# A bf16 head that also prepares fp16 weights: one scale for each half of w's columns, with the work on w dealt out anew between ScalarE and VectorE

## The chip, the cores and the metric

The kernel runs on one core of a Trainium2 chip. The core has a matrix engine (TensorE, PE in the profile; its weight loads are PEld), VectorE (DVE), ScalarE (ACT), GpSimd (POOL) and SyncE (SP, which here only issues DMAs). The metric is the time of one execution on the device in microseconds.

## The reference

```
B, S, D = 8, 2048, 2048          # x: (B, S, D) and w: (D, D), float32, normal draws
cs = np.cumsum(x, axis=1)
diff = cs - np.concatenate([zeros, cs[:, :-1, :]], axis=1)
return np.matmul(diff, w).astype(np.float32)
```

The difference of a running sum with itself, one step back, is x again, so the kernel computes the product of x, as 16384 rows of 2048, with w.

## The kernel before, in words

The 16384 rows are 128 row tiles of 128. All but the first four are multiplied in fp16 by a Winograd scheme (seven block products in place of eight, on two levels for most of the work), whose block sums need x and w scaled to fp16. The scheme is not part of the change; what it needs of w is. In its four blocks, B11 and B21 are the upper and lower row halves of w's left 1024 columns, B12 and B22 those of the right 1024; T1 to T4 are differences of the blocks.

**The head.** While w arrives, the first four row tiles (PLAIN = 4) are multiplied plainly in bf16, so that TensorE has work. w comes as 32 tiles of 128 rows by 1024 columns, float32, 512 KB each: `fetch(h, ko)` loads tile ko (0 to 15) of column half h, first all of the left half, then all of the right. x's four row tiles come in four quarters of 512 columns (`load_x`), placed between the loads of w; `cast_x` turns a quarter into bf16 in two instructions on VectorE, `turn_x` transposes it on TensorE into PSUM bank 7, eight 128x128 transposes for two row tiles at a time, and `turned` copies the result out. In the lists `loads` and `turns`, quarters 1, 2 and 3 are loaded ahead of tiles 2, 5 and 9, and turned at tiles 2 and 3, 5 and 6, 9 and 10.

`taken(h, ko)` does two things with a tile of w that has landed: ScalarE casts it to bf16 into one of seven ring buffers `wb` (L259), and VectorE takes the largest magnitude of each partition (L262). `plain(h, r, ko)` multiplies row tile r with it (L275), one 512-column matmul for each PSUM bank, seven for a tile of the left half, eight for the right: bank 7 is needed for the transposes, so the eighth product of the left half is left for later. The last four tiles (KQ = 4) of each half are run row by row, so that `plain_out` can copy a finished row's banks out on ScalarE (L295) while the next row is multiplied. The right half uses the same banks, so its first tile waits for those copies. AHEAD = 3 right-half tiles are fetched and cast before this.

**The scale.** When all 32 tiles are in, VectorE reduces the 32 maxima (L366), GpSimd takes the maximum over the partitions (L367, `partition_all_reduce`), and two small VectorE instructions give uw and its reciprocal uinv (L369, L371). GpSimd then issues seven stores (`put`, L285) for finished rows. `block` turns a float32 tile of w, in place, into a scaled fp16 tile: VectorE does it for B11, B21 and B12 (L382), 24 instructions, ScalarE for most of B22 (L386).

**Rows of x in the scheme.** For each row tile t, `weigh` takes row sums of magnitudes on ScalarE (L123, two 1024-column instructions, each with a read of the accumulator), `scale_of` turns them into a scale on VectorE (L139, L141), `unit_of` multiplies it by uw on GpSimd (L147), `narrow` casts the scaled row to fp16 on ScalarE (L158), and `turn` transposes it by DMA (L171). `keep` on ScalarE (L581) and `add` on VectorE (L584) bring a product out of PSUM, times the row tile's unit, into an output buffer.

**Order.** `after` chains every instruction behind the last one on its engine, so each engine runs in the order in which the Python code calls the helpers, and an instruction that waits holds up all that follow on that engine. Between the engines only the data count. Behind the head stand, on ScalarE: the row sums and the narrowing of row tile 4, the copies of row 0 (banks 0 and 1), the row sums of tile 6, the copies of row 1 (banks 2 and 3), and so on. TensorE goes on with `left_over(bank(2))`, the 16 matmuls of the product that was left (L400), into bank 2, and then with the scheme (L554, L573). Row tile 5 is loaded into xP's space once rows 0 and 1 are done with it (L432).

**The end.** The last group's final products are run in the order written out in END_ORDER: in its last line a bank q is closed by P4.p7, then read by `add.C21h1.q` on VectorE and by `keep.C21h0` on ScalarE; the last add, `add.C21h0.x`, needs that keep's result.

Of the kernel before, what the change touches and what calls it, by code (L numbers as in the profile page):

```python
# [10 lines left out]
def kernel(  # L11
# [6 lines left out]
    nc = tc.nc  # L18
# [23 lines left out]
    PLAIN = 4  # L42
    KQ = KO // 4
# [26 lines left out]
    uw = const.tile([P, 1], f32, name="uw")  # L70
    uinv = const.tile([P, 1], f32, name="uinv")
# [60 lines left out]
    def scale_of(t):  # L132
        if t < END:
            m2 = sums_of.pop(t)
            m, s, u = (m2[:, i : i + 1] for i in (2, 3, 4))
# [44 lines left out]
    with ExitStack() as head:  # L180
# [10 lines left out]
        wmax = first.tile([P, 2 * KO], f32, name="wmax")  # L191
        wred = first.tile([P, 1], f32, name="wred")
# [62 lines left out]
        def taken(h, ko):  # L255
            wt = whole[ko % KH][:, ko // KH, h, :]
            i = h * KO + ko
            b = wb[h, ko] = turn_of(ring)
            after("act", lambda: nc.scalar.copy(b, wt))  # L259
            after(  # L260
                "dve",
                lambda: nc.vector.tensor_reduce(  # L262
                    wmax[:, i : i + 1], wt, AX.X, MAX, apply_absolute_value=True
                ),
            )

# [31 lines left out]

        for i in range(WARM):
# [6 lines left out]
        AHEAD = 3  # L306
# [59 lines left out]
        after("dve", lambda: nc.vector.tensor_reduce(wred, wmax, AX.X, MAX))  # L366
        whole_max = nc.gpsimd.partition_all_reduce(uw, wred, P, bass_isa.ReduceOp.max)  # L367
        after(
            "dve", lambda: nc.vector.tensor_scalar(uw, uw, TINY, 1.0 / TOP, MAX, MUL)  # L369
        )  # L370
        after("dve", lambda: nc.vector.reciprocal(uinv, uw))  # L371
# [4 lines left out]


        def block(dst, a, h, k, engine):
            src = whole[k][:, a, h, :].rearrange("p (n c) -> p n c", c=NB)
            if engine == "dve":  # L380
                after(
                    "dve", lambda: nc.vector.tensor_scalar(dst[k], src, uinv, None, MUL)  # L382
                )
            else:
                after(
                    "act", lambda: nc.scalar.activation(dst[k], src, COPY, scale=uinv)  # L386
                )
# [8 lines left out]
        def left_over(ps):  # L396
# [12 lines left out]
            after("act", lambda: nc.scalar.activation(c, ps, COPY, scale=uw))  # L409
# [3 lines left out]
        for k in range(4):  # L413
            block(B11, 0, 0, k, "dve")
# [23 lines left out]
        for k in range(4, KH):  # L438
# [809 lines left out]
```

## Time and profile before

| | |
|---|---|
| median of 3 runs | 1454.4 us (1453.6 to 1454.54) |
| profiled execution | 1453.86 us, of which the span from the first to the last instruction is 1452.1 us |
| granted TensorE clock | 1.000 over the span |
| busy share of the span | PE 99%, DVE 92%, ACT 67%, POOL 3% |
| DMA | 351.59 MB, 242 GB/s on the mean; 404 GB/s from 10 to 20 us |
| chain that ended last | PE 96%, DMA 2%, DVE 1% of the span |

The profiled execution lies inside the three runs; 1.8 us of it are outside the span. Times inside the profile are counted from the span's start. A row of the timeline gives the start, the length, the engine, the line in the code, the operation, what it writes and reads, the shape and how many instructions are merged into the row; in brackets stands how long the engine was idle before it and what ended that. A matmul's record is 0.38 us long, but the next one starts before it ends, so rows of matmuls are counted by their starts. An engine's neighbouring instructions overlap by about 0.09 us in the same way.

### The profile page before, as it was taken

To read this page: it belongs to the slowest core of one execution; us is meant where nothing else is said; L and a number is where in the kernel's file an instruction comes from. 1 tells how busy PE (TensorE), PEld (TensorE's weight loads), DVE (VectorE), ACT (ScalarE), POOL (GpSimd) and SP (SyncE) were. 2 spreads that over 40 slices of the span, in tenths; PEclk is the share of its full clock that TensorE was granted. 3 is DMA by queue.
4 is the path that set the end of the run, shared out by engine and by line. 5 is a ranking of instruction groups with operands and counts; after the bars stand their busy time and mean duration, and the time that the engine had idled before them with its cause. 6 is when DMAs were issued, how large, how long until landed. Compare 5 with 4: busy or idle time off the path is not lost.

```text
span 1452.1 us, 20113 instructions
## 1 busy us (share of the span) xinstructions
PE 1438.4 (99%) x6673; PEld 651.6 (45%) x6679; DVE 1332.9 (92%) x2301; ACT 967.7 (67%) x1446; POOL 47.2 (3%) x136
## 2 busy tenths in 40 slices
PE   8999999999999999999999999999999999999998
PEld 3444444444444444444444444444444444444443
DVE  7998999999999999999999999999999999999998
ACT  5887566776666676666666667666667766666662
POOL 0111000000000000000000000000000000000000
PEclk9999999999999999999999999999999999999999
DMA  9999788898888888888898888998878898888983
GB/s 363 370 237 299 194 220 240 239 261 235 231 238 231 250 245 235 233 238 237 249 253 225 232 236 234 265 235 239 229 231 244 249 235 239 222 245 246 252 203 123
DMA packets 377752, 351.59 MB, mean 242 GB/s; under 512 B 274800, under 2 KB 274800, under 8 KB 377520
## 3 DMA queue, kind: packets, MB, share of 16 engines
q1 hardware_dynamic: 377088, 348.47, 84.9%
q0 software_dynamic: 560, 1.84, 0.4%
q8 instruction: 52, 0.85, 0.2%
q14 instruction: 52, 0.43, 0.1%
HBM read 150.99 MB, written 134.22 MB: 196 GB/s over the span
## 4 chain that ended last, share of the span: by engine, by line
PE 96%; DMA 2%; DVE 1%; ACT 0%; issue 0%; SPq 0%; ACTq 0%
PE b L573 61%; PE b L554 33%; PE b L275 2%; DMA W<-in_w_dram 2%; DVE c L584 1%; DMA W<-in_x_dram 0%; ACT wb L259 0%; PE b L400 0%; ACT o L295 0%; SPq L219 0%; ACT c L581 0%; SPq L253 0%; DVE x L544 0%; ACTq L259 0%
## 5 line engine op out<-in xcount | busy, mean ns | idle before, releaser
L584 DVE SCALAR_TENSOR_TENSOR c<-b,of,c 128x512 f32<-128x512 f32 x790 | 573.9, 747 | 73.1 <-PE b L573 62.5
L554 PE MATMUL b<-W,x 128*128 128x512 f16 x2144 | 506.6, 379 | 0.0
L581 ACT ACTIVATE c<-b,of 128x512 f32<-128x512 f32 x492 | 312.6, 680 | 227.3 <-PE b L573 115.7
L573 PE MATMUL b<-W,x 128*128 128x512 f16 x1904 | 454.9, 379 | 0.0
L158 ACT ACTIVATE F<-F,of 128x1024 f16<-128x1024 f32 x246 | 282.2, 1147 | 175.4 <-DVE of L141 173.2
L573 PEld LDWEIGHTS <-x 128*128 128x128 f16 x2500 | 244.6, 98 | 295.7 <-issue 1.5
L554 PEld LDWEIGHTS <-x 128*128 128x128 f16 x2144 | 209.8, 98 | 253.0
L123 ACT ACTIVATE waste<-F 128x1024 uint8<-128x1024 f32 x246 | 259.3, 1054 | 4.9 <-DMA F<-in_x_dram 2.8
L573 PEld LDWEIGHTS <-inner 128*128 128x128 f16 x1644 | 160.9, 98 | 194.0
L573 PE MATMUL b<-W,inner 128*128 128x512 f16 x940 | 241.2, 379 | 0.0
L544 DVE TENSOR_TENSOR x<-x,x 128x1024 f16<-128x1024 f16 (+1 forms) x390 | 227.4, 583 | 3.2
L573 PE MATMUL b<-flow,x 128*128 128x512 f16 x588 | 150.9, 379 | 0.0
L573 PE MATMUL b<-inner 128*128 128x512 f16 x472 | 121.1, 379 | 0.0
L895 DVE TENSOR_TENSOR flow<-W 128x2048 f16<-128x2048 f16 x88 | 107.0, 1216 | 0.0
L988 DVE TENSOR_TENSOR b<-b,c 128x512 f32<-128x512 f32 x116 | 80.6, 695 | 13.5 <-PE b L573 13.4
L147 POOL TENSOR_SCALAR of<-of,uw 128x1 f32<-128x1 f32 x124 | 42.0, 357 | 1305.4 <-DVE of L139 703.1
L895 DVE TENSOR_TENSOR flow<-W,inner 128x2048 f16<-128x2048 f16 x58 | 70.8, 1221 | 0.0
L981 ACT COPY c<-b 128x512 f32<-128x512 f32 x58 | 33.4, 576 | 52.2 <-PE b L573 49.6
L275 PE MATMUL b<-wb,xP 128*128 128x512 bf16 x234 | 55.1, 383 | 6.6 <-ACT wb L259 5.2
L544 DVE TENSOR_TENSOR inner<-x 128x512 f16<-128x512 f16 x117 | 49.4, 422 | 2.9 <-DMA x<-F 0.9
L981 ACT COPY b<-b 128x512 f32<-128x512 f32 x87 | 51.2, 588 | 0.0
L544 DVE TENSOR_TENSOR inner<-x,inner 128x512 f16<-128x512 f16 x117 | 49.3, 421 | 2.0
(61 smaller groups left out, 524.3 us busy)
## 6 DMA issues: line engine op xcount, KB each, us to landing
F<-in_x_dram SPq DMA_DIRECT2D x246, 512.0 KB, 5.1
out_dram<-c SPq DMA_DIRECT2D x492, 256.0 KB, 3.0
W<-in_w_dram SPq DMA_DIRECT2D x32, 512.0 KB, 9.7
W<-in_x_dram SPq DMA_DIRECT2D x16, 256.0 KB, 7.3
x<-F SPq DMA_TRANSPOSE x246, 3.3
out_dram<-o POOLq DMA_DIRECT2D x5, 256.0 KB, 4.1
out_dram<-o SPq DMA_DIRECT2D x5, 256.0 KB, 3.4
xP<-in_x_dram SPq DMA_DIRECT2D x1, 1024.0 KB, 5.1
```

The costliest lines, as they stand in the source:

```text
L123: lambda: nc.scalar.activation(waste, where[t][i], ABS, scale=1.0 / ROW, accum_out=sums_of[t][:, i : i + 1],),
L147: after("pool", lambda: nc.gpsimd.tensor_scalar(u, m, uw, None, MUL))
L158: lambda: nc.scalar.activation(narrowed(t)[:, ds(i * NH, NH)], where[t][i], COPY, scale=s),
L275: lambda: nc.tensor.matmul(ps[r][n], xP[:, r, ko, :], wb[h, ko][:, ds(n * NB, NB)], start=(ko == 0), stop=(ko == KO - 1),),
L544: after("dve", lambda: nc.vector.tensor_tensor(dst.all, p.all, q.all, op))
L554: said = nc.tensor.matmul(to[n], a[k], b[k][:, n, :], start=(first and k == 0), stop=(k == KH - 1), skip_group_check=True,)
L573: said = nc.tensor.matmul(to, a[k], b[k], start=(first and k == 0), stop=(k == 3), skip_group_check=True)
L581: after("act", lambda: nc.scalar.activation(c, p, COPY, scale=u))
L584: after("dve", lambda: nc.vector.scalar_tensor_tensor(c, p, u, c, MUL, ADD))
L895: after("dve", lambda: nc.vector.tensor_tensor(in_twos(flow), x, y, op))
L981: after("act", lambda: nc.scalar.copy(c, p))
L988: after("dve", lambda: nc.vector.tensor_tensor(t, p, s, ADD))
```

## The change

w's two column halves get a scale each. It comes no longer from the largest magnitude but from the largest row sum of magnitudes of a 1024-column row, over 2048, and ScalarE makes the sums (`measure`, an ACTIVATE with an accumulator into `wsum`, in the form of `weigh`). VectorE casts w to bf16, but for the first two tiles (EARLY = 2), and also does all copies of transposed x out of PSUM. `scale_of_w(h)` runs once for each half: for the left one as soon as its 16 tiles are in. With that scale, `turn_left` turns one tile of B11 or B21 to fp16 on VectorE behind each right-half cast. AHEAD falls from 3 to 1, and the left half's last two tiles, not four, are run row by row. The row tiles' units become two columns, one for each half of w, and keeps and adds take the one for their output's columns. In END_ORDER `keep.C21h0` goes ahead of `add.C21h1.q`. The lines that only rename a unit are left out below.

```diff
+    EARLY = 2
-    uw = const.tile([P, 1], f32, name="uw")
-    uinv = const.tile([P, 1], f32, name="uinv")
+    uw = const.tile([P, 2], f32, name="uw")
+    uinv = const.tile([P, 2], f32, name="uinv")
...
-            after("pool", lambda: nc.gpsimd.tensor_scalar(u, m, uw, None, MUL))
+            after("pool", lambda: nc.gpsimd.tensor_scalar(u, uw, m, None, MUL))
...
-        def taken(h, ko):
+        def cast(h, ko):
             wt = whole[ko % KH][:, ko // KH, h, :]
-            i = h * KO + ko
             b = wb[h, ko] = turn_of(ring)
-            after("act", lambda: nc.scalar.copy(b, wt))
+            if h == 0 and ko < EARLY:
+                after("act", lambda: nc.scalar.copy(b, wt))
+            else:
+                after("dve", lambda: nc.vector.tensor_copy(b, wt))
+
+        def measure(h, ko):
+            wt = whole[ko % KH][:, ko // KH, h, :]
             after(
-                "dve",
-                lambda: nc.vector.tensor_reduce(
-                    wmax[:, i : i + 1], wt, AX.X, MAX, apply_absolute_value=True
+                "act",
+                lambda: nc.scalar.activation(
+                    waste,
+                    wt,
+                    ABS,
+                    scale=1.0 / TOP,
+                    accum_out=wsum[:, h, ko : ko + 1],
                 ),
             )
+
+        def taken(h, ko):
+            cast(h, ko)
+            measure(h, ko)
+
+        def scale_of_w(h):
+            u, v, m = (t[:, h : h + 1] for t in (uw, uinv, wtop))
+            after("dve", lambda: nc.vector.tensor_reduce(m, wsum[:, h], AX.X, MAX))
+            said = nc.gpsimd.partition_all_reduce(u, m, P, bass_isa.ReduceOp.max)
+            after("dve", lambda: nc.vector.tensor_scalar(u, u, TINY, None, MAX))
+            after("dve", lambda: nc.vector.reciprocal(v, u))
+            return said
...
-        AHEAD = 3
+        AHEAD = 1
...
-        for ko in range(KO - KQ):
+        casts, weights = list(range(KO)), list(range(KO))
+
+        def cast_to(ko):
+            while casts and casts[0] <= ko:
+                cast(0, casts.pop(0))
+
+        def measure_to(ko):
+            while weights and weights[0] <= ko:
+                measure(0, weights.pop(0))
+
+        for ko in range(KO - 2):
             if ko == 0:
                 for a in range(2):
                     xb = cast_x(0, [a])
                     turned(0, a, turn_x(xb, a, 6 + a), "dve")
                     if a == 0:
-                        taken(0, ko)
+                        cast_to(EARLY - 1)
                     for r in (2 * a, 2 * a + 1):
                         plain(0, r, ko)
                 continue
+            cast_to(ko)
             if ko in turns:
                 q, a = turns[ko]
                 if a == 0:
                     xb = cast_x(q)
                 v = turn_x(xb, a, 7)
-                taken(0, ko)
-                turned(q, a, v, "act")
-            else:
-                taken(0, ko)
+                cast_to(ko + 1)
+                turned(q, a, v, "dve")
+            measure_to(ko - 0)
             for r in range(PLAIN):
                 plain(0, r, ko)
-        for ko in range(KO - KQ, KO):
-            taken(0, ko)
+        cast_to(KO)
+        measure_to(KO)
         for ko in range(AHEAD):
             fetch(1, ko)
+        for r in range(PLAIN):
+            for ko in range(KO - 2, KO):
+                plain(0, r, ko)
+            plain_out(0, r)
+        scale_of_w(0)
         for ko in range(AHEAD):
             taken(1, ko)
-        for r in range(PLAIN):
-            for ko in range(KO - KQ, KO):
-                plain(0, r, ko)
-            plain_out(0, r)
...
+        left = [(B, a, k) for a, B in enumerate((B11, B21)) for k in range(KH)]
+
+        def turn_left(n):
+            for _ in range(min(n, len(left))):
+                B, a, k = left.pop(0)
+                block(B, a, 0, k, "dve")
+
         for ko in range(KO - KQ):
             if ko >= AHEAD:
                 fetch(1, ko)
                 taken(1, ko)
+                turn_left(1)
             for r in range(PLAIN):
                 plain(1, r, ko)
...
         for ko in range(KO - KQ, KO):
             taken(1, ko)
+            turn_left(1)
...
-        for k in range(4):
-            block(B11, 0, 0, k, "dve")
+        turn_left(KH)
         weigh(PLAIN)
         scale_of(PLAIN)
         unit_of(PLAIN)
-        for k in range(4, KH):
-            block(B11, 0, 0, k, "dve")
         narrow(PLAIN)
         turn(PLAIN)
+        for k in range(KH):
+            block(B12, 0, 1, k, "dve")
         finish_row(0)
-        for k in range(4):
-            block(B21, 1, 0, k, "dve")
...
     END_ORDER = """
     P4.p1 keep.C21g0 P4.p5 keep.C21g1 P4.p6 add.C21g1.q keep.C21h1 P4.p2
     add.C21g0.x put.C21g0 P4.p3 add.C21h1.e add.C21g1.x put.C21g1 P4.p7
-    add.C21h1.q keep.C21h0 put.C21h1 P4.p4 add.C21h0.x put.C21h0
+    keep.C21h0 add.C21h1.q put.C21h1 P4.p4 add.C21h0.x put.C21h0
     """.split()
```

More of the change, by code (lines that the diff above doesn't have):

```diff
@@ L190 @@
         eye = first.tile([P, P], bf16, name="eye")
-        wmax = first.tile([P, 2 * KO], f32, name="wmax")
-        wred = first.tile([P, 1], f32, name="wred")
+        wsum = first.tile([P, 2, KO], f32, name="wsum")
+        wtop = first.tile([P, 2], f32, name="wtop")
         zeros = xP[:, 0, :KQ, :].rearrange("p k m -> p (k m)")
@@ L296, in plain_out, with block @@
                 done.append((c, ds(r * P, P), ds(h * NH + n * NB, NB)))
+        def block(dst, a, h, k, engine):
+            src = whole[k][:, a, h, :].rearrange("p (n c) -> p n c", c=NB)
+            if engine == "dve":
+                after(
+                    "dve", lambda: nc.vector.tensor_scalar(dst[k], src, uinv[:, h : h + 1], None, MUL)
+                )
+            else:
+                after(
+                    "act", lambda: nc.scalar.activation(dst[k], src, COPY, scale=uinv[:, h : h + 1])
+                )
         for i in range(WARM):
@@ L365 @@
             load(t, 1)
[L366 to L371, printed above, removed]
+        whole_max = scale_of_w(1)
         with tc.issue_after(whole_max.ins):
@@ L375 @@
         done = []
[L378 to L387, printed above, removed]
         def finish_row(r):
@@ L437 @@
         finish_row(2)
-        for k in range(4, KH):
-            block(B21, 1, 0, k, "dve")
         weigh(PLAIN + 1)
         finish_row(3)
-        for k in range(5):
-            block(B12, 0, 1, k, "dve")
-        for k in range(5, KH):
-            block(B12, 0, 1, k, "dve")
         scale_of(PLAIN + 1)
@@ L741, in group_plain @@
         C21 = pair()
[L742 removed]
+        keeps(C21, Y, kh)
         narrow(h + 5)
@@ L1018, in some @@
             def some():
-                add(self.at[c], self.at[b], unit[self.row(c)])
+                add(self.at[c], self.at[b], self.unit(c))
                 self.close(b, let)
@@ L1132, in plan @@
             self.add("C21h1", q, "q")
-            self.keep("C21h0", q, let=True)
+            self.keep("C21h0", q, let=tiles["g"] + 4 < END)
             self.quarter("P4", "p4", h0, False)
```

48 lines of the change are left out of this document (27 added, 21 removed).

## The prediction

> **What bounds the kernel now.** Read first: each engine's busy share, on the page.
>
> ```profile
> PE 1438.4 (99%) x6673; PEld 651.6 (45%) x6679; DVE 1332.9 (92%) x2301; ACT 967.7 (67%) x1446; POOL 47.2 (3%) x136
> ```
>
> TensorE is busy in 1438.4 of 1452.1 us, so a gain can come only from the 13.7 us in which it idles or from what stands behind its last matmul. Where these lie is read from TensorE's timeline (start, length, line, work, count, idle time before it).
>
> ```profile
> 28.80 0.61 PE L238 MATMUL b<-eye,W 128*128 128x128 bf16 x8
> 30.06 1.67 PE L275 MATMUL b<-wb,xP 128*128 128x512 bf16 x7 [0.65 <-ACT wb L259]
> ...
> 38.00 33.50 PE L275 MATMUL b<-wb,xP 128*128 128x512 bf16 x147 [0.35 <-ACT wb L259]
> 71.34 3.62 PE L400 MATMUL b<-W,xP 128*128 128x512 f16 x16
> ```
>
> Up to 38 us the matmuls wait for ScalarE's casts of w. The leftover block (L400) starts at 71.34 and its 16 matmuls take until 74.80, the next product's start: 0.216 us each. After it no idle row of TensorE is left until the end. One more loss is inside the 33.50 us row; the chain of waits, in order of time, shows it as ScalarE's copies (L295) from 43.36 to 44.98, and then (start, length, what):
>
> ```profile
> 45.01 2.32 PE b L275 x10
> ```
>
> The matmuls of the right half's first w tile wait, one by one, for the copies out of the seven banks; the seventh starts at 45.01, so that tile ends two slots later, at 45.44. From there 15 tiles of 8 matmuls, 120 x 0.216 = 25.9 us, reach 71.34: no slack. ScalarE's timeline and then VectorE's give what the moved work costs.
>
> ```profile
> 42.41 2.55 ACT L295 COPY o<-b 128x512 f32<-128x512 f32 x5
> ...
> 60.45 1.05 ACT L123 ACTIVATE waste<-F 128x1024 uint8<-128x1024 f32 x1
> 61.41 0.19 ACT L123 ACTIVATION_READ_ACCUMULATOR waste<-F 128x1 f32 x1
> 61.63 1.06 ACT L123 ACTIVATE waste<-F 128x1024 uint8<-128x1024 f32 x1
> ...
> 66.15 1.07 ACT L295 COPY wb<-b 128x512 f32<-128x512 f32 x2 [0.56 <-PE b L275]
> ...
> 69.35 0.57 ACT L295 COPY wb<-b 128x512 f32<-128x512 f32 x1
> ```
>
> ```profile
> 12.64 1.28 DVE L229 CAST W<-W 128x1024 bf16<-128x1024 f32 x2
> ...
> 28.91 19.18 DVE L262 TENSOR_REDUCE wmax<-W 128x1 f32<-128x1024 f32 x15 [0.59 <-DMA W<-in_w_dram]
> ```
>
> A row sum of magnitudes (L123) is issued every 61.63 - 60.45 = 1.18 us, its accumulator read included. A VectorE cast of this size is 0.69 us, and two take 1.28, so the second costs 0.59 more. The reductions start as w lands: tile 9 of the left half at 28.9, then one each 19.18 / 15 = 1.28 us, so tile 15 at 36.6.
>
> **The change, part by part.** *Left half, casts.* From tile 2 on VectorE casts, 0.69 us behind a landing in place of ScalarE's 1.05. But its queue now holds the cast of tile 9 ahead of the two casts of x's last quarter. The first of these ends at 28.91 + 1.28 = 30.19, where before all of x's casts were done by 28.3; the eight transposes start at 30.24 and not at 28.80, and tile 9's matmuls 0.45 us later, at 30.69 instead of 30.06: 0.6 us lost. (Earlier quarters lose the same way, but tile 8's matmuls still end at about 28.8, before 30.24, so that is covered by the wait for tile 9.) From 30.69 nothing is late: the copy-out of x behind the cast of tile 10 still frees bank 7, for the next transposes, at 32.0, before tile 9's matmuls end at 32.20; tiles 10 to 15 are cast 0.7 us behind their landings, tile 15 at 37.3, against its first use at 39.1. Seven tiles of seven matmuls (49 x 0.216 = 10.57) and one more set of transposes (0.45) end the left half at 30.69 + 11.02 = 41.71.
>
> *Banks.* Only the last two tiles, not four, are now run row by row. Row 0 is then finished at 39.5 and ScalarE, whose row sum of tile 15 ended at 36.6 + 1.18 = 37.8, copies seven banks out at a pitch of (2.55 - 0.65) / 4 = 0.475 us (the last copy 0.65): the seventh starts at 42.39 and ends at 43.04. The seventh matmul of the right half starts at 43.08, against 45.01. TensorE is 1.9 us ahead, and ready for L400 at 43.08 + 0.43 + 25.9 = 69.4.
>
> *The left half's scale.* A new wait: VectorE reduces the sums at 37.8, POOL takes the maximum over the partitions, two small operations follow. The same four steps before took from 58.63 to 59.72, 1.09 us; so 38.9. Queued behind it on VectorE is the right half's first cast (ends at 39.6), for which TensorE comes at 41.71: covered by 2.1 us. Fetching ahead one tile and not three moves no DMA: the queue waits for landings, and only the fourth right-half tile waits for transposes that end 0.7 us later, with seven others still under way.
>
> *Right half on VectorE.* Per tile a cast and one left block to fp16 (L382: 2.74 us for four, a pitch of 0.66): 1.26 us, under the landing's 1.28 and far under TensorE's 8 x 0.216 = 1.73. Sixteen blocks thus leave the stretch after 60 us, some 10.6 us of VectorE.
>
> *Right half on ScalarE.* Here it gives back. Behind the seventh copy (42.39 + 0.475 = 42.87) stand 16 row sums: 16 x 1.18 = 18.9, to 61.75. Before, its casts let go at 60.45: 1.3 us late now, and x's first row sums, its narrowing, and the copies are queued behind. Before, ScalarE waited for row 0 until 66.15 though its narrowing had ended at 65.59 (overlap of neighbours 0.09), so 0.65 of the lateness is absorbed. The copy that frees bank 2 (69.35 to 69.92) then runs from 70.0 to 70.57. L400 writes bank 2, so it starts at 70.6 and not at TensorE's 69.4: a new stall of 1.2 us, and of the 1.9 us there stay 71.34 - 70.62 = 0.72. Next late would be bank 2 again, copied from L400's result (80.42 to 81.09, wanted at 81.70 less 0.72 = 80.98). Its narrowing waited 1.41 us for VectorE, which is free earlier now, so ScalarE's own queue decides: 0.65 of lateness on the work up to 76.78 ends that copy at about 80.3. (x's reload, L432, goes out behind two later transposes, some 0.9 us after its 68.08, and with 5.1 us lands at 74.1, when its row sum, 73.48 before, comes due.) The rest of the order is unchanged and VectorE is earlier everywhere, so 0.72 is kept.
>
> *The last output.* Bank q is read by a VectorE add and a ScalarE scaling, one after the other; the diff swaps them.
>
> ```profile
> 1443.29 4.04 DVE L584 SCALAR_TENSOR_TENSOR c<-b,of,c 128x512 f32<-128x512 f32 x6
> ...
> 1445.61 1.03 PE L573 MATMUL b<-flow,x 128*128 128x512 f16 x4
> 1447.36 0.69 ACT L581 ACTIVATE c<-b,of 128x512 f32<-128x512 f32 x1 [3.90 <-DVE c L584]
> 1448.08 0.75 DVE L584 SCALAR_TENSOR_TENSOR c<-b,of,c 128x512 f32<-128x512 f32 x1 [0.76 <-ACT c L581]
> ```
>
> ScalarE sat idle 3.90 us for the sixth add. First in order, it starts when bank q's last matmul is out (the next bank's began at 1445.61; 1445.8) and ends at 1446.5, just as the sixth add begins (1443.29 + 5 x 0.66 = 1446.58). The last add follows at 1447.24, not 1448.08: 0.84. Bounds: nothing if the sixth add is held back equally, 0.84 at most.
>
> *POOL's queue.* The second maximum comes at 62.1, not 58.96, 3.1 late, and so do its puts: the first reused buffer's, issued at 60.69, lands by 60.69 + 3.1 + 4.1 = 67.9, before ScalarE writes it at 70.5. L147's products follow at 74.8, wanted by keeps at 84.11 - 0.72. Covered.
>
> *Two scales elsewhere.* POOL's products become 128x2; L147 took 0.36 us on the mean with 1305 us idle before it. Keeps and adds read another column. Nothing.
>
> **Sum.** 1453.86 us for the profiled execution (span 1452.1 and 1.8 around it) less 0.72 and 0.84 is 1452.3. The median shown is 0.54 above that execution, so 1452.8.
>
> The unknown is the row sum over w, whose nearest rows are L123 (1.18) and the casts (8.84 us for nine at 44.79: 0.96 without an accumulator read); from above, the landing's 1.28. I take 1.18, the same operation. At 0.96 or so ScalarE is 3.5 us earlier and the stall is gone; at 1.28 it is 1.6 later.
>
> The Trainium skill ("ScalarE: Activation LUTs", What ACT_TABLE_LOAD costs) gives 186 ns + 0.833 per element for an ACTIVATE with immediate scale and an overlap of 93 ns between neighbours, an estimate of 0.95 us here; the casts agree, the row sums at 1.18 do not, and by that rule alone the time would be the first rival's.
>
> **The rivals.**
> 1. *Nothing is given back.* Row sums at the casts' pitch: L400 at 69.4, gain 1.9 + 0.84 = 2.75, 1451.6. Against it, 246 accumulator reads of 0.19 us.
> 2. *All is given back.* Row sums at 1.28: bank 2 is free at 72.2, 0.9 later than now; with the end's 0.84 the time is 1454.4, no change. For it: VectorE and 400 GB/s of DMA work on the same tile as ScalarE; against: L123's extremes in the whole run are 1.039 and 1.070.
> 3. *Slower: POOL's first maximum.* Another program is loaded on POOL after its last put (64.0), and its next work starts at 71.69: 7.7 us. If the left half's maximum paid this at 38 us, the first right-half cast would end 7.7 us late, at 47.3; TensorE would end that tile at 49.0 against 45.44, 3.6 late, less 0.84: 1457.2. It decides from 5 us on (2.1 of cover, 1.9 and 0.84 of gain). Against it: the load stands at the program's start, and at 58.96 the maximum took 0.38.
>
> The Trainium skill ("GPSIMD Engine Reference", 2.1 Instruction dispatch) says that the first call of a freshly loaded kernel pays about 6 us more; the 7.7 us agree in kind, the 0.38 us maximum does not, and by the rule the third rival holds.
>
> **How the numbers follow.** Forecast 0.58, rival 1 0.13, rival 2 0.15, rival 3 0.08, something unseen 0.06. The runs shown spread by 0.94 us, so a change under 0.2%, 2.9 us, can't be told from none. Rival 1 lies just short of that: half of it and some of the unseen make faster 0.10; rival 3 and the rest of the unseen, slower 0.10; same 0.80. The range goes from rival 1 less half the spread, 1451.1, to rival 2 and the way towards rival 3, 1455.2.
>
> **What would show it.** Right: transposes at 30.2 and no TensorE wait from there to about 43; row sums on ScalarE from 43 to 62 at 1.18; a TensorE wait of some 1.2 us before the leftover block, released by ScalarE's copy; that block at 70.6; the last VectorE add straight behind the sixth. Wrong: a leftover block at 69.4 or after 71.3, TensorE waiting on VectorE at 42, POOL's maximum over 2 us, or idle rows on TensorE after 75 us.

## The result, and the profile after

| | before | after |
|---|---|---|
| median | 1454.64 us (15 runs, 1453.6 to 1455.13) | 1457.53 us (15 runs, 1456.63 to 1458.75) |
| profiled execution | 1453.86 us, span 1452.1 us | 1457.86 us, span 1456.1 us |
| ratio | | 1.0020, 95% interval 1.0013 to 1.0028 |

The change made the kernel slower by 2.9 us on the medians, outside the predicted range (1451.1 to 1455.2). In the rows below b is a PSUM bank; F, o, wb and x are buffers, in which, among other things, finished rows wait for their stores. Of the profile after, first TensorE's timeline (start, length, line, work, count, idle time before it and what ended that):

```profile
31.83 0.62 PE L243 MATMUL b<-eye,W 128*128 128x128 bf16 x8 [2.04 <-DVE W L234]
...
72.31 3.61 PE L440 MATMUL b<-W,xP 128*128 128x512 f16 x16 [1.11 <-ACT wb L321]
75.76 3.62 PE L585 MATMUL b<-W,x 128*128 128x512 f16 x16
81.06 10.79 PE L585 MATMUL b<-W,x 128*128 128x512 f16 x48 [1.68 <-ACT o L321]
93.22 3.63 PE L585 MATMUL b<-W,S 128*128 128x512 f16 x16 [1.37 <-DVE S L575]
```

The leftover block (L400 before, L440 now) has the predicted stall. Behind it stand two more waits, at 81.06 and 93.22 us, where before had none. Start by start the 4.0 us between the two spans are found: the leftover block is 0.97 late (72.31 against 71.34); the matmuls that began at 75.76 are through at 79.2, so the wait costs 1.84, and the next matmul starts 0.49 later and not 0.22, as it needs the second of the two copied banks, whose copy ends at 81.49; the wait at 93.22 costs 1.5; the end gives back 0.63. That is 0.97 + 1.84 + 0.27 + 1.5 - 0.63 = 3.95.

Who let TensorE wait at 81.06 is read from ScalarE's timeline:

```profile
61.09 1.06 ACT L272 ACTIVATE waste<-W 128x1024 uint8<-128x1024 f32 x1
...
62.27 1.06 ACT L272 ACTIVATE waste<-W 128x1024 uint8<-128x1024 f32 x1
...
71.69 0.57 ACT L321 COPY wb<-b 128x512 f32<-128x512 f32 x1
...
78.20 1.06 ACT L124 ACTIVATE waste<-xP 128x1024 uint8<-128x1024 f32 x1 [2.27 <-DMA xP<-in_x_dram]
...
80.44 1.05 ACT L321 COPY o<-b 128x512 f32<-128x512 f32 x2
```

The row sums of w come at their 1.18 us, and the copy at 71.69 ends the first stall. Then ScalarE sits idle for 2.27 us, for the reload of xP's space with row tile 5. Only behind that tile's row sums stand the two copies at 80.44 for which TensorE waits. The reload is SyncE's. In the profile of before, GpSimd's first stores and SyncE's queue (start, length, work; a DMA's row ends when it is issued, not when it lands; landing times below are from the same traces):

```profile
59.22 1.48 POOL L285 DMA_DIRECT2D out_dram<-F  x2
```

```profile
64.43 3.23 SPq L171 DMA_TRANSPOSE x<-F  x2
68.08 0.34 SPq L432 DMA_DIRECT2D xP<-in_x_dram  x1
```

and in that of after, and GpSimd's timeline of after:

```profile
67.44 5.16 SPq L176 DMA_TRANSPOSE x<-F  x2
72.70 0.57 SPq L469 DMA_DIRECT2D xP<-in_x_dram  x1
```

```profile
39.63 0.38 POOL L288 PARTITION_ALL_REDUCE uw<-wtop  x1 [39.20 <-DVE wtop L287]
63.73 0.35 POOL L288 PARTITION_ALL_REDUCE uw<-wtop  x1 [23.71 <-DVE wtop L287]
63.95 1.86 POOL L311 DMA_DIRECT2D out_dram<-F  x2
```

Row tile 4's two transposes hold SyncE's queue for 5.16 us, before for 3.23, and they start 3.0 us late, so the reload goes out 4.6 us late, and lands at 78.18 where it was 73.17. Beside them are the seven stores that GpSimd issues behind the second maximum. Before, the first store went out 5.2 us ahead of the first transpose (59.22 and 64.43); now it is 3.5 (63.95 and 67.44), and the transposes land at 74.89 and 75.08, with the last store (74.70).

The end of the program, on VectorE and ScalarE:

```profile
1447.91 4.70 DVE L615 SCALAR_TENSOR_TENSOR c<-b,of,c 128x512 f32<-128x512 f32 x7
1450.43 0.69 ACT L612 ACTIVATE c<-b,of 128x512 f32<-128x512 f32 x1 [2.35 <-PE b L604]
```

The last seven adds run in one piece, as predicted.

### The profile page after: what moved, and what is told of

The parts are those of the page before. It is cut to its first block, busy times and chain, and to the rows that moved or that the text cites. A ratio compares the mean times of both kernels' runs of the same rounds, so it can differ in the third digit from the quotient of the medians.

```text
span 1456.1 us, 20180 instructions
## 1 busy us (share of the span) xinstructions
PE 1439.7 (99%) x6679; PEld 651.7 (45%) x6679; DVE 1317.0 (90%) x2308; ACT 969.9 (67%) x1474; POOL 46.9 (3%) x137
## 3 DMA queue, kind: packets, MB, share of 16 engines
q0 software_dynamic: 560, 1.84, 0.4%
## 4 chain that ended last, share of the span: by engine, by line
PE 93%; DMA 2%; issue 2%; DVE 1%; ACT 1%; SPq 0%; DVEq 0%; ACTq 0%
PE b L604 61%; PE b L585 32%; DMA W<-in_w_dram 1%; PE b L301 1%; DVE c L615 1%; DMA W<-in_x_dram 0%; DMA xP<-in_x_dram 0%; SPq L224 0%; ACT waste L124 0%; DVE W L488 0%; ACT waste L272 0%; DVE wb L266 0%; DVE W L329 0%; ACT wb L321 0%; DVE W L567 0%
## 5 line engine op out<-in xcount | busy, mean ns | idle before, releaser
L575 DVE TENSOR_TENSOR x<-x,x 128x1024 f16<-128x1024 f16 (+1 forms) x390 | 227.1, 583 | 3.2
L1021 DVE TENSOR_TENSOR b<-b,c 128x512 f32<-128x512 f32 x116 | 80.4, 693 | 13.4 <-PE b L604 13.4
L149 POOL TENSOR_SCALAR of<-uw,of 128x2 f32<-128x2 f32 x124 | 41.1, 346 | 1305.6 <-DVE of L141 724.7
L575 DVE TENSOR_TENSOR inner<-x 128x512 f16<-128x512 f16 x117 | 49.2, 421 | 3.1 <-DMA x<-F 1.1
L575 DVE TENSOR_TENSOR inner<-x,inner 128x512 f16<-128x512 f16 x117 | 49.2, 421 | 2.0
```

Source lines behind the costliest of these rows:

```text
L149: after("pool", lambda: nc.gpsimd.tensor_scalar(u, uw, m, None, MUL))
L575: after("dve", lambda: nc.vector.tensor_tensor(dst.all, p.all, q.all, op))
L1021: after("dve", lambda: nc.vector.tensor_tensor(t, p, s, ADD))
```

## The experiments

Theory S: the stores' traffic holds row tile 4's transposes, these hold SyncE's queue, and x's reload behind them comes too late. Theory A: ScalarE is late by its row sums, and that alone makes all three waits.

### After, unaltered

> The changed kernel once more, unaltered. Theory S (SyncE's queue): GpSimd's seven stores, moved behind the second maximum, share the DMA engines with the two transposes of row tile 4, which then hold SyncE's queue (issues of 1.85 and 3.21 us where they were 1.41 and 1.72), so the reload into xP is issued at 72.70 and not at 68.08, and the TensorE waits of 1.68 us at 81.06 and of 1.37 us at 93.22 follow from it. Theory A (ScalarE alone): ScalarE is late by its 16 row sums and everything behind the head is only that lateness. Both expect the three TensorE waits again (about 1.1, 1.7 and 1.4 us). Open: whether the first tile of w lands 1.2 us later than in the kernel before (8.24 against 7.03) because of the change or by chance; if by chance, it lands anywhere from 7.0 to 8.3 here.

One execution, 1457.1 us. The w tiles landed otherwise (the first at 7.81 us, not 8.24; tile 9 of the left half at 29.33, not 30.38), and the profile shows what part of the loss that is. TensorE's timeline and then SyncE's queue:

```profile
71.27 3.61 PE L440 MATMUL b<-W,xP 128*128 128x512 f16 x16 [1.13 <-ACT wb L321]
...
80.35 12.26 PE L585 MATMUL b<-W,x 128*128 128x512 f16 x48 [2.01 <-ACT o L321]
```

```profile
66.40 5.32 SPq L176 DMA_TRANSPOSE x<-F  x2
71.83 0.71 SPq L469 DMA_DIRECT2D xP<-in_x_dram  x1
```

The leftover block starts at 71.27, behind a stall of 1.13, and so 0.07 us earlier than in before: the 0.97 of the first profile was late w. The wait at 80 us is there again, the one at 93 is not, and the row behind the wait at 80 is 12.26 us long for 48 matmuls, not 10.79. The same execution in stretches (length; busy time of PE, PEld, DVE, ACT, POOL; then the granted clock, the DMA share and GB/s):

```profile
78.00:82.00 4.00, 1.99 (x6) 0.56 (x5) 2.10 (x6) 3.94 (x8) 1.37 (x1) 0.80 1.20 212
82.00:86.00 4.00, 4.00 (x16) 1.65 (x15) 4.00 (x8) 4.00 (x5) 0.00 (x0) 0.77 1.06 274
```

The granted clock falls to 0.80 and 0.77: after 2.0 us without work eight matmuls start 0.43 us apart and not 0.216, which costs 8 x 0.21 = 1.7 us on top of the wait.

### Half the row sums of the right half

```diff
...
-            measure(h, ko)
+            if h == 0 or ko % 2 == 0:
+                measure(h, ko)
...
```

> The right half's scale is taken from every second tile only, eight row sums in place of sixteen; the sums of the other eight are left out. ScalarE is free 5 us earlier (near 58.5, the last landing and one row sum), the second maximum and the stores come near 59 as they did before the change. Theories S and A both expect the three waits behind the head to vanish and a time of 1452 to 1453.5 us, 4 to 5.5 under the changed kernel and 1 to 2.5 under the one before. A third view, that the row sums have nothing to do with it and the rest of the change (casts and blocks on VectorE, two maxima) costs the time, expects at least 1456.5.

The right half's eight sums are also packed together, and the maximum is taken over those eight. 1453.34 us (1453.08 to 1454.51) beside a before of 1454.33, measured alongside; ratio to before 0.9995, 95% interval 0.9985 to 1.0004. TensorE:

```profile
70.23 3.62 PE L441 MATMUL b<-W,xP 128*128 128x512 f16 x16
...
88.48 3.63 PE L586 MATMUL b<-W,S 128*128 128x512 f16 x16 [0.40 <-DVE S L576]
```

No stall at the leftover block, and behind it the 0.4 us at 88 and another 0.4 in short waits inside the row of 64 matmuls before it (14.41 us long, in before 13.98). The view that the rest of the change costs the time fell, and the lateness of the sums is what the loss starts from. The run doesn't tell S from A, since the maximum, and so the stores, come earlier too. It does show that a held queue isn't enough: here too the transposes hold SyncE for 5.07 us, from 63.49, but the reload goes out at 68.67, and the time is not above before's.

### The stores behind the left half's maximum

```diff
-        scale_of_w(0)
+        left_max = scale_of_w(0)
+        with tc.issue_after(left_max.ins):
+            for c, rows, columns in done:
+                put(c, rows, columns)
+        done = []
...
-        whole_max = scale_of_w(1)
-        with tc.issue_after(whole_max.ins):
-            for c, rows, columns in done:
-                put(c, rows, columns)
-        done = []
+        scale_of_w(1)
```

> GpSimd's seven stores go out behind the left half's maximum (near 44 us, when their copies are done) and not behind the second one. Theory S: the transposes of tile 4 have the DMA engines to themselves, issue in about 1.4 and 1.7 us and land some 4 us after; the reload goes out by 71; the waits at 81 and 93 shrink to 0.4 us or less together, the wait ahead of the leftover block stays near 1.1; 1454 to 1455.2 us. Theory A: the waits stay at 1.7 and 1.4 us, 1457 to 1458. For both, stores beside the loads of w can make the right half's tiles land up to 4 us later; a TensorE wait before 60 us would show that.

1456.61 us (1455.45 to 1458.5); ratio 1.0016, 1.0007 to 1.0025: neither theory's number. The trace says why:

```profile
72.81 5.21 PE L440 MATMUL b<-W,xP 128*128 128x512 f16 x16 [2.60 <-ACT wb L321]
77.86 13.98 PE L585 MATMUL b<-W,x 128*128 128x512 f16 x64
```

Both late waits are gone, as S says: the row of 64 matmuls runs without a break to 91.7, the transposes hold SyncE for 2.71 us and the reload lands at 76.30. But TensorE also begins this row 3.1 us later than in after unaltered (77.86, not 74.72), which alone would cover a wait of 2.0, so the missing waits don't decide between S and A. For the stores now share the DMA engines with w, whose last tile lands at 62.49 and not at 58.37 us; ScalarE's sums end 1.4 us later for it, the stall grows from 1.1 to 2.6, and TensorE's clock is halved for eight matmuls (16 matmuls take 5.21 us). The stores' 1.84 MB are some 4.5 us of DMA, an estimate at the 410 GB/s that before reaches from 30 to 40 us; the last tile lands 4.1 us later.

### The reload ahead of row tile 4's transposes

```diff
         narrow(PLAIN)
-        turn(PLAIN)
...
         after("sp", lambda: nc.sync.dma_start(x5, x2[ds((PLAIN + 1) * P, P), :]))
+        turn(PLAIN)
```

> On SyncE's queue the reload into xP is issued ahead of the two transposes of tile 4. Theory S: it goes out when TensorE is done with rows 0 and 1 (67 to 68 us) and lands by 74; the waits at 81 and 93 go; the transposes land some 1 to 2 us later than 75.1 and the first product behind the leftover block may wait that much; 1454 to 1456 us. Theory A: the row sums of tile 5 begin no earlier than ScalarE's own queue allows and the time stays at 1457 to 1458.

1456.87 us (1456.67 to 1458.18); ratio 1.0018, 1.0008 to 1.0028.

```profile
75.92 7.08 PE L585 MATMUL b<-W,x 128*128 128x512 f16 x32 [1.19 <-DMA x<-F]
84.08 7.08 PE L585 MATMUL b<-W,x 128*128 128x512 f16 x32 [1.08 <-DMA x<-F]
```

A miss that teaches, again between the two theories' times: the wait for ScalarE's copies is gone, but TensorE now waits for the transposes themselves, landed behind stores and reload (75.87 and 76.78), and for those of row tile 6 after that (84.03 and 84.87). In both orders what stands second in SyncE's queue is late, so the order alone isn't the fault.

### After without the seven stores

```diff
-        with tc.issue_after(whole_max.ins):
-            for c, rows, columns in done:
-                put(c, rows, columns)
         done = []
```

> After without the seven stores that GpSimd issues behind the right half's maximum (the left halves of rows 0 to 3 are not written). Theory S (the stores' packets hold row tile 4's transposes, these hold SyncE's queue, the reload is late): the two transposes hold SyncE for about 1.4 and 1.7 us and not 1.8 and 3.3, the reload goes out within 3.8 us of the first one's issue (after: 5.3), TensorE's waits at about 81 and 93 us are gone or under 0.3 us, the 1.1 us stall at the leftover block stays; 1453.5 to 1454.8. Theory A (ScalarE's lateness alone): the waits stay, 1456.5 to 1457.5.

1453.71 us (1452.97 to 1455.23) beside a before of 1454.6; ratio 0.9995, 0.9986 to 1.0003. SyncE's queue, TensorE's timeline and ScalarE's:

```profile
66.41 2.71 SPq L176 DMA_TRANSPOSE x<-F  x2
69.22 0.52 SPq L466 DMA_DIRECT2D xP<-in_x_dram  x1
```

```profile
71.28 3.61 PE L437 MATMUL b<-W,xP 128*128 128x512 f16 x16 [1.09 <-ACT wb L321]
74.72 13.98 PE L582 MATMUL b<-W,x 128*128 128x512 f16 x64
```

```profile
61.24 1.06 ACT L272 ACTIVATE waste<-W 128x1024 uint8<-128x1024 f32 x1
...
74.78 1.07 ACT L124 ACTIVATE waste<-xP 128x1024 uint8<-128x1024 f32 x1
```

This is the run that decides, beside the unaltered one above. ScalarE is late by the same amount in both: its last sum ends at 62.30 (62.29 there), the stall is 1.09 (1.13), row tile 4's transposes go out at 66.41 (66.40). Only the stores differ. Without them the transposes hold SyncE for 2.71 us and not for 5.3, the reload lands at 74.53 and not at 77.47, ScalarE doesn't wait for it, TensorE has no wait at 80 (nor at 93, where the first profile had one), and 3.4 us of time are gone. A, that ScalarE's lateness alone makes the waits, fell; S stands, with that lateness as its start.

### Before with late stores

```diff
...
+        for _ in range(6):
+            with tc.issue_after(whole_max.ins):
+                whole_max = nc.gpsimd.partition_all_reduce(
+                    idle, wred, P, bass_isa.ReduceOp.max
+                )
         with tc.issue_after(whole_max.ins):
```

> Before, with six more maxima over the partitions on GpSimd, written to a place that nobody reads, between the maximum and the seven stores: at 0.38 us each the stores go out some 2 us later, and nothing else is moved (SyncE's order, ScalarE and VectorE are those of before). Row tile 4's first transpose then goes out some 3.2 us behind the first store and not 5.2 (after: 3.5). Theory S: the two transposes hold SyncE 1.8 and 3 us and land behind the stores, the reload goes out 1.5 to 3 us later than in before, TensorE waits for ScalarE's copies at 78 to 81 us, and the time is 1455.5 to 1458. Theory A (only ScalarE's sums make it late): before's time within 0.4 us, no wait of TensorE after 46 us.

1459.67 us (1457.83 to 1462.02), above both theories' times; ratio 1.0039, 1.0025 to 1.0052. GpSimd, SyncE and TensorE, a fence each:

```profile
60.23 5.75 POOL L375 PARTITION_ALL_REDUCE idle<-wred  x6
```

```profile
68.82 0.82 SPq L438 DMA_DIRECT2D xP<-in_x_dram  x1
```

```profile
81.71 12.16 PE L560 MATMUL b<-W,x 128*128 128x512 f16 x48 [2.56 <-ACT o L296]
```

The six maxima took 5.75 us and not 2.3, so the stores are 6.1 us later than in before (65.36 for 59.22; after: 4.7), more than was meant, and row tile 4's transposes go out with the first of them and hold SyncE for 2.7 us. The reload, issued 0.7 us later than in before, then takes 10.0 us to land, not 5.1, at 78.84, among the stores; its row sums start at 78.86 on ScalarE, and the same wait of TensorE at 81 appears, with the half clock behind it. ScalarE also sits idle for 3.5 us before 74.21, for an output buffer whose store landed at 74.13, so two ways in which a late store can hurt are in this number. Either alone would have held the row sums to about the same time: the copy in front of them ends at 78.47, the reload lands at 78.84. The run shows that late stores alone, with every other instruction as in before, cost 5 us by the medians; in the profiled execution 0.7 of that is late w (the leftover block starts at 72.08). It doesn't show S's own link, transposes that hold SyncE's queue, and the share of each way stays open.

### The swap at the end alone

```diff
...
-    add.C21h1.q keep.C21h0 put.C21h1 P4.p4 add.C21h0.x put.C21h0
+    keep.C21h0 add.C21h1.q put.C21h1 P4.p4 add.C21h0.x put.C21h0
```

> Before, with only the swap in the written-out end (the keep ahead of the sixth add, its bank let go by the add). The prediction's term: the last add starts straight behind the sixth, 0.84 us earlier, so 1453.5 beside a before of 1454.3. Rival: the sixth add is held back by as much as the keep is moved forward, and the time is before's.

1453.62 us (1453.2 to 1454.12) beside 1454.6; ratio 0.9994, 0.9985 to 1.0003. The medians are 0.98 apart, which the interval doesn't tell from nothing. The trace does: the last add ends 1.35 us behind the last matmul's end, in before 2.20, so the step's 0.84 is there. But the span ends 4.83 us behind the last matmul's end, in before 5.46: 0.63. The last store now follows the one before it by 0.66 us, not 1.51, and takes 2.54 us to land in place of 2.32. The same distances, 4.81 to 4.84 us with the swap and 5.46 without, stand in every other trace that stores the whole result.

### Before once more, for its first loads

> Before, unaltered, for the spread of its first loads. In the runs so far the first w tile landed at 7.03 us (before), 8.24, 7.81, 7.20, 7.86 and 7.79 (after and its variants). If that is chance, it lands anywhere from 7.0 to 8.3 here, and with it everything up to 71 us, but TensorE still has no wait between 46 us and the end. If the changed code makes the first loads later, it lands at 7.0 to 7.1.

1453.7 us; the first tile of w landed at 7.16 us, the last at 57.14. In the kernel with the swap alone, whose head is that of before, these were 7.97 and 58.49. The profiled executions with after's head and its order of stores lie from 7.20 to 8.36 and from 57.29 to 58.49. So most of the 1.1 us by which w came late in the first profile of after is the spread of the loads. That the change has no part in it is not shown: tile 9 of the left half landed from 28.71 to 29.34 in four executions with before's head, and from 28.94 to 30.38 in ten with after's.

### x's casts first in the left half

```diff
+            if ko in turns and turns[ko][1] == 0:
+                xb = cast_x(turns[ko][0])
             cast_to(ko)
             if ko in turns:
                 q, a = turns[ko]
-                if a == 0:
-                    xb = cast_x(q)
```

> After with the two casts of each quarter of x ahead of the cast of the w tile that follows them in VectorE's order. The prediction's first step (the casts of x stand behind the cast of tile 9): the last quarter's first transpose starts before tile 9 has landed (before: 0.1 us before, after: 1.45 us after), and tile 9's matmuls some 0.75 us behind its landing. As the stall at the leftover block is set by ScalarE, it grows by what TensorE gains, and the time stays after's, 1456.6 to 1458. If the transposes wait for something else, they start 1.4 us behind the landing as in after.

1455.56 us, one execution, below the range expected. TensorE:

```profile
70.15 3.61 PE L440 MATMUL b<-W,xP 128*128 128x512 f16 x16 [1.09 <-ACT wb L321]
...
90.92 3.63 PE L585 MATMUL b<-W,S 128*128 128x512 f16 x16 [1.00 <-DMA out_dram<-o]
```

Tile 9 landed at 28.94, its matmuls start 1.13 us later, at 30.07; in the two executions of after it was 1.9, in before 1.17. The queueing of x's casts is confirmed, at 0.7 us for the predicted 0.6. The expectation that the stall eats what TensorE gains was wrong: the stall is 1.09, as good as unchanged, and the leftover block is 1.1 us earlier than in after unaltered, 0.4 of it because tile 9 landed earlier. ScalarE's sums of the right half stand behind the left half's copies, which TensorE releases, so the whole chain moved with it (last sum at 61.18, not 62.29). That 1.5 us came off the span rests on one execution, in which the wait at 79 us was 1.91 us and the clock stayed whole. The second row names what the S differences wait for: a store of the head's results.

### Three of the sums on VectorE

```diff
...
+        shared = (3, 6, 9)
...
+            if h == 1 and ko in shared:
+                after(
+                    "dve",
+                    lambda: nc.vector.tensor_reduce(
+                        wsum[:, h, ko : ko + 1], wt, AX.X, ADD, apply_absolute_value=True
+                    ),
+                )
+                return
...
-                turn_left(1)
+                if ko not in shared and ko - 1 not in shared:
+                    turn_left(1)
```

> After, with three of the right half's sixteen row sums (tiles 3, 6 and 9) given to VectorE as sums of magnitudes, and six of its fp16 blocks left for later in return; the whole result is computed. If ScalarE's sixteen sums are the root: ScalarE's last sum ends within 1.4 us of the last landing (after: 4.8), no stall at the leftover block over 0.3 us, under 0.6 us of waits behind it, 1452.8 to 1453.6, below before. Rival: VectorE's reductions hold its casts back and TensorE waits for them before 60 us; then 1455 or more.

1454.14 us (1453.08 to 1456.03), above the range expected; ratio 0.9998, 0.9989 to 1.0006. ScalarE's last sum ends at 58.94, 1.1 us behind the last landing, and yet the leftover block waits 1.24 us. ScalarE's timeline:

```profile
65.51 2.33 ACT L163 ACTIVATE F<-F,of 128x1024 f16<-128x1024 f32 x2 [3.91 <-DVE of L143]
```

The fp16 blocks that were left for later stood ahead of row tile 4's scale in VectorE's order, so narrowing waited 3.9 us for it: one queue's lateness had been moved to another. The run is also a second test of S and A, with all stores in place. GpSimd's stores and SyncE's queue:

```profile
60.02 1.95 POOL L320 DMA_DIRECT2D out_dram<-F  x2
```

```profile
66.68 2.72 SPq L176 DMA_TRANSPOSE x<-F  x2
69.50 0.52 SPq L479 DMA_DIRECT2D xP<-in_x_dram  x1
```

Row tile 4's transposes are as late as in after unaltered (66.40 there), but the stores went out 6.7 us ahead of them and not 3.5. The transposes hold SyncE for 2.72 us, and TensorE has no wait near 80 us. Mended:

```diff
-        turn_left(KH)
         weigh(PLAIN)
+        turn_left(1)
         scale_of(PLAIN)
         unit_of(PLAIN)
+        turn_left(KH)
```

> The version with three row sums on VectorE, but row tile 4's scale goes ahead of the six fp16 blocks that were left for later (there they held the scale back until 65.1 us, ScalarE idle 3.9 us for it, and the 1.2 us stall stayed). Now row tile 4 is narrowed from about 62 us, the copy that frees bank 2 ends before 70 us, and the leftover block has no stall over 0.3 us: 1452.8 to 1453.6. If the stall stays over 1 us, ScalarE's sums were not its cause.

1453.58 us (1452.9 to 1456.08), as expected, beside a before of 1454.52; ratio 0.9995, 0.9986 to 1.0004.

```profile
69.80 3.62 PE L450 MATMUL b<-W,xP 128*128 128x512 f16 x16
...
77.19 10.57 PE L596 MATMUL b<-W,x 128*128 128x512 f16 x48 [0.32 <-ACT o L330]
```

The stall is gone, so ScalarE's sums were its cause; two waits stay, 0.32 at 77 and 0.82 at 88 us. With x's casts first, and T1's differences ahead of row tile 5's scale on VectorE:

> The mended version, and with it x's casts first in the left half and the eight differences T1 ahead of row tile 5's scale on VectorE. TensorE should come to the leftover block about 1 us earlier than in the mended version, and keep some of it: 1452.0 to 1453.2. If the next waits (row tile 4's transposes, or the S differences that wait for stores) take it back, it is within 0.3 us of the mended version.

1453.6 us (1452.6 to 1455.43), no better than the version before it; ratio 0.9994, 0.9986 to 1.0003.

```profile
77.55 10.57 PE L596 MATMUL b<-W,x 128*128 128x512 f16 x48 [0.98 <-ACT o L330]
```

The wait at 88 is gone, but the one at 77 grew to 0.98: what TensorE gains ahead of the reload, it waits for behind it. In both kernels the transposes and the stores still overlap, and the transposes hold SyncE for 4.7 and 4.8 us; they are only some 4 us earlier than in after. Neither version, nor the swap alone, is told from before by its interval, and by the medians both have no more (0.9 us) than the swap alone has (1.0).

## Why the prediction was wrong, step by step

*Left half, casts:* right. The transposes started 1.45 us behind tile 9's landing (31.83 and 30.38), for the predicted 30.24 - 28.89 = 1.35.

*Banks:* right. Between the last transposes of x and the leftover block TensorE has no idle row (170 matmuls in one row of 36.96 us from 34.24 on); the right half's first tile no longer waits.

*The left half's scale:* right, and the third rival, the slower one, fell: the first maximum took 0.38 us at 39.63, no program load in front of it. That this rival's time, 1457.2, lies near the measured 1457.5 is chance.

*Right half on VectorE:* right; casts start 1.27 us apart (42.17 and 43.44), for 1.26.

*Right half on ScalarE:* right in size. Sums at 1.18 us (61.09 and 62.27), the last one over at 63.3 and 62.3 in the two executions for 61.75, 1.6 and 0.5 us late, with tile 9 of the left half, from which the chain runs, landing 1.5 and 0.4 us later than in before; a stall of 1.11 and 1.13 for 1.2. This disposes of the rivals on the row sum's price.

*The failed step* is the bracket in *Right half on ScalarE*, "x's reload, L432, goes out behind two later transposes, some 0.9 us after its 68.08, and with 5.1 us lands at 74.1", with the "Covered" of *POOL's queue*. The stores' 3.1 us were reckoned, and checked only against the buffers that they free. That they share the DMA engines with the transposes was not looked at: both steps took the lengths of before and shifted them. By the prediction's own numbers the stores came 3.1 late and the reload behind the transposes 0.9, so the 5.2 us between first store and first transpose had to shrink by some 2. The runs put in its place: transposes that hold SyncE 5.2 to 5.3 us in place of 2.7 to 3.2, a reload that goes out at 71.8 to 72.7 and lands at 77.5 to 78.2, ScalarE idle for it, its copies of row 3 from 79.7 and 80.4 on, and TensorE idle for 1.7 to 2.0 us.

Two things had to come together. With the queue held for 5.07 us, but everything some 3 us earlier (half the sums), nothing was lost against before: 1453.34 us. With row tile 4's transposes as late as in after unaltered, but the queue held for 2.7 us (no stores, and three sums on VectorE), nothing was lost either: 1453.71 and 1454.14 us. Without the stores the reload went out at 69.22 and landed at 74.53, near the 69.0 and 74.1 of the prediction; the other steps then left 1453.71 us, 0.9 over the forecast, with the leftover block at 71.28 for 70.62, as tile 9 had landed 0.5 us later than in before.

From there two more losses follow that no step named. When TensorE's idle time reached 2.0 us, the clock was halved for eight matmuls, 1.7 us in the second execution. And the S differences (L575) wait for the later stores of SyncE's queue, out of memory that they are to write: in the first profile one of these stores, issued at 88.61, landed at 92.29, 0.18 us before VectorE went on, and TensorE idled for 1.37 us. The two losses were not seen in one execution: the one with the half clock had no wait at 93. VectorE's timeline of the first profile:

```profile
80.57 0.21 DVE L141 TENSOR_SCALAR of<-of 128x1 f32<-128x1 f32 x1 [8.34 <-ACT waste L124]
...
92.47 0.69 DVE L575 TENSOR_TENSOR S<-x,x 128x1024 f16<-128x1024 f16 x1 [2.44 <-issue]
```

The sentence "The rest of the order is unchanged and VectorE is earlier everywhere, so 0.72 is kept" fell with it. VectorE is earlier, but sits 8.34 us idle before 80.57, at row tile 5's scale, with T1's differences queued behind.

*The last output:* the mechanism was right, and 0.84 is what the last add gained. The term was mis-sized in the span, 0.63, since the last store lands 0.22 later behind its closer neighbour.

## What to carry to other kernels

When a step moves work on an engine, ask of every DMA behind it not only whose buffer it frees, but which other transfers it will now run beside: two groups of transfers that were 5.2 us apart were 3.5 apart after the change, and the queue held for that, on top of the engine's lateness, cost what neither cost alone. Where the queue that waits also issues the next loads, follow it to the first consumer. And a repair that moves work from a late engine to a free one must also look at what stands behind it there: three sums moved to VectorE left a stall of 1.24 us at the leftover block until row tile 4's scale had been put ahead of the blocks that they displaced.

## What the runs showed of the hardware that was not expected

*The clock.* Waits of TensorE of 1.1 to 1.9 us (1.11, 1.13, 1.19, 1.68, 1.91) left the matmuls behind them at 0.216 us, at most one at 0.49, which needs the second copied bank. Waits of 2.01, 2.56 and 2.60 us were each followed by eight matmuls mostly 0.43 us apart, 3.4 us in all, and then by full pace. One wait of 2.04 us in the head, ahead of transposes, shows no such stretch, so the limit isn't the length alone. (Longer waits, of up to 2.78 us, stand ahead of the clock's first rise, which the traces put at 11 to 18 us.) The Trainium skill ("TensorE: Matmul & The Clock Gate", Part 1) tells of a gate that halves the clock after an idle window of about 3.4 us and opens it after a busy one of that length, the windows running freely. The trace agrees on the half rate and on the 3.4 us until it opens; the idle time that closed it here was 2.0 us, under the window.

The traces also show what decides. In each of the 14, every change of the clock comes a whole number of 3.41 us behind its first rise: after unaltered, the clock fell 20 such stretches behind the rise and was half for one. Some of these stretches, as above (length, PE's busy time first, the clock behind POOL's), from after unaltered, from x's casts first and from the first profile of after:

```profile
77.01:80.42 3.41, 1.40 (x8) 0.55 (x6) 0.53 (x3) 2.89 (x6) 0.25 (x1) 1.00 1.05 303
80.42:83.83 3.41, 3.41 (x9) 1.09 (x9) 3.41 (x7) 3.38 (x5) 1.12 (x1) 0.50 1.23 156
```

```profile
75.64:79.05 3.41, 1.58 (x8) 0.59 (x7) 0.38 (x3) 2.74 (x6) 0.33 (x2) 1.00 1.27 304
79.05:82.46 3.41, 3.22 (x15) 1.40 (x15) 3.41 (x6) 3.38 (x6) 1.26 (x1) 1.00 1.02 165
```

```profile
26.82:30.23 3.41, 2.97 (x14) 1.18 (x12) 0.00 (x0) 0.00 (x0) 0.00 (x0) 1.00 1.01 402
30.23:33.65 3.42, 1.82 (x15) 1.12 (x16) 3.18 (x6) 2.93 (x5) 0.00 (x0) 1.00 1.03 410
```

The half clock follows exactly the three stretches in which TensorE was busy least, for 0.95, 0.98 and 1.40 us of 3.41; behind the next ones, with 1.58, 1.73 and 1.82, it stayed whole. So a wait counts by how much of it falls into one stretch: the 2.04 us of the head, from 29.79 to 31.83, were cut in two at 30.23, the 2.01 us from 78.34 to 80.35 were not. Where between 1.40 and 1.58 us the limit lies was not measured.

*Transposes beside stores.* Two DMA transposes held SyncE's queue for 2.7 us alone and for 5.2 to 5.3 us while GpSimd's stores were under way, and landed 7.5 and 5.7 us after issue in after, 3.3 and 3.1 without the stores. The distance from the first store to the first transpose goes with the hold: 6.7 us apart 2.7, 5.2 apart 3.1 and 3.2 (before, twice), 3.1 to 3.6 apart 4.7 to 5.3 (six executions). In before with late stores, where the first transpose went out 0.2 us ahead of the first store, the hold was 2.7 us, though the second transpose landed only 7.4 us after issue. The Trainium skill ("DMA: Bandwidth & Descriptors", Queues, rings and completion order) says that each DMA engine takes turns between its queues, packet by packet. The trace agrees: the stores are slowed too, the last two landing 2.4 and 1.3 us behind one another, where those before came every 0.7 to 1.1.

*GpSimd.* Six maxima in a row took 0.42 to 1.24 us each, one alone 0.35 to 0.38.
